# Attention's weight pieces prepared in DRAM during the first ConvFFN, and the queries' swaps issued from ScalarE's queue

## The chip, the cores and the metric

The kernel runs on one core of a Trainium2 chip. The metric is the device time of one execution in microseconds (us), and of several executions the median. Engines are named as in the profile: PE is TensorE, DVE VectorE, ACT ScalarE, POOL GpSimd, and SP is SyncE, which does nothing here but issue DMAs.

## The reference

It is one step of a small decoder over 16 meta tokens, 1024 prompt tokens and 8 sample tokens, with 1024 features: a pooling mixer and a ConvFFN, one shared projection to keys and values, sliding-window attention with sinks, and a second ConvFFN. All is fp32.

```python
def conv_ffn(xs, prefix, w_in, conv_w, conv_b, w_out):
    gu = xs @ w_in                                  # 1024 -> 2 x 2816
    g, u = gu[..., :D_FF], gu[..., D_FF:]
    gp = jnp.concatenate([prefix.astype(g.dtype), g], axis=1)
    c = conv_b
    for k in range(CONV_W):                         # 3 taps
        c = c + gp[:, k:k + S] * conv_w[k]
    h = jax.nn.silu(c) * u
    return h @ w_out, gp[:, -(CONV_W - 1):]
...
    q = (x @ w_q + b_q).reshape(B, L, N_KV_HEADS, GROUP, HEAD_DIM)   # 16 heads of 64
    o = sink_attention(q, k_band, v_band, mask[None, :, None, None], sinks)
    return o @ w_o + b_o
```

## The kernel before

**Exact halves.** An fp32 operand is kept as two parts, a rounded one (hi) and the rest (lo), and a product is made of three matmuls (`mm3`, L116 to L122): hi by hi, hi by lo, lo by hi. Weights arrive in DRAM unsplit. `load_w` (L103) loads 512 KB on SP's queue into one of two `raw` buffers, ACT rounds it into the first half of `w` (L111, CAST), and POOL subtracts (L112) into the second half. Weights of the FFN are split in one piece of 1024 columns, those of the queries (`wq`) and of the output projection (`wo`) in two of 512.

**Stages.** Tokens are columns, in three chunks: 280 columns (meta, samples and 256 of the prompt), 384 and 384. The stages are the mixer (to about 120 us), ConvFFN 1 (about 85 to 840 us, the two interleave), the shared keys and values (about 840 to 890 us), attention (to about 1215 us), and ConvFFN 2 (to the end).

**ConvFFN.** For each of 22 feature tiles f and each chunk c, `ffn1(f, c)` makes the gate product `pg` and the other product `pu` (24 matmuls each); ACT copies `pg` out (`g`, L374 to L376 or L390), POOL and DVE make the convolution (L392 to L394), ACT applies Silu (L398), DVE multiplies by `pu` (L399), ACT rounds the result to `h` (L401) and DVE makes its rest (L402). After f = 3, 4, 6, 8, ... `ffn2(gi, c)` multiplies two tiles of h by `w_wo`, eight products `po` for each chunk; DVE adds them up (for the first group L417 and L418, which also take in the residual; later L420).

**PSUM.** Six banks go round among all these products. A bank that held `pg` comes free when ACT has copied it, one that held `pu` when DVE has multiplied by it. In ffn2 that follows ffn1(f, 2), the first four `po` take the banks of chunks 0 and 1, the fifth takes that of `pg` and the sixth that of `pu` of chunk 2.

**Attention.** For each of 3 chunks and 8 pairs of heads, a query projection `pq` (24 matmuls, L607, spread over the units of the pair before) ends in `Q.finish` (L611 to L628): ACT writes hi of both heads into `q1` (L622), DVE writes lo into `q2` (L627), and since each head also needs the other part in the other 64 partitions, four DMAs swap them, issued on SP's queue (L623 behind ACT, L628 behind DVE). Then each unit of 128 tokens runs scores `s` (PE, L639 and L640), a masked minimum (DVE, L645), exp (ACT, L647), a scale by the reciprocal sum (DVE, L650), a transpose `tp` three units later (PE, L658), its split into `ring` (ACT L660, DVE L661), and the product with the values `av` five units later (PE L676), split into `o` (ACT L681, DVE L683). The output projection `pz` (o_piece, L748) runs beside later units. Eight weights of `wq` and eight of `wo` are needed by every chunk; each chunk loads and splits them again, 48 times in all.

**Order.** Each engine runs its instructions in a fixed order, which a scheduler has set when the program was built; an instruction that waits holds up all behind it on its engine, and a DMA is issued in the order of the engine that issues it. The tag `lt` has five buffers for temporaries of the layer norms, which are idle while the FFN runs.

Of the kernel before, what the change touches and what calls it, by code (L numbers as in the profile page):

```python
# [13 lines left out]
P = 128  # L14
# [13 lines left out]
# prompt blocks (of 128 tokens) per chunk; the first chunk also carries the  # L28
# meta tokens and the sample tokens: columns [meta 16 | samples 8 | prompt]
# [6 lines left out]
# columns alive after the attention: [meta14 meta15 | samples 8 | prompt]  # L36
# [3 lines left out]
# packed per-partition constant columns  # L40
# [7 lines left out]
# constants of the first phase alone  # L48
# [6 lines left out]
def r32(ap):  # L55
    return ap.bitcast(F32)
# [3 lines left out]
def trunk_kernel(ctx: ExitStack, tc: tile.TileContext, ins: dict, outs: dict):  # L60
# [19 lines left out]
    # ------------------------------------------------------------ constants  # L80
# [33 lines left out]

    def mm3(out, wts, movs):
        """out += sum_k w_k^T x_k over exact hi/lo parts (all but lo*lo)."""  # L116
        n = len(wts)
        for k in range(n):
            (wh, wl), (mh, ml) = wts[k], movs[k]
            nc.tensor.matmul(out, lhsT=wh, rhs=mh, start=(k == 0), stop=False)  # L120
            nc.tensor.matmul(out, lhsT=wh, rhs=ml, start=False, stop=False)  # L121
            nc.tensor.matmul(out, lhsT=wl, rhs=mh, start=False, stop=(k == n - 1))  # L122
# [7 lines left out]
    # ----------------------------------------------------------- layer norm  # L130
    def colsum(parts, W, name, on_pe, own=False, split=False, pairs=False, step=KT):
        """mean over all features of 8 [P, W] tiles -> PSUM, on every partition; pauses after every step tiles."""
        ps = bank(f"ps_{name}", "ln")[:, :W]
        if on_pe:
            # fp32 products; with pairs, of sums of two tiles
            n = KT // 2 if pairs else KT
            for k in range(n):
                if pairs:
                    t = hslot([P, W], f"pr{k}_{name}", F32)
                    (nc.gpsimd if k < n // 2 else nc.vector).tensor_tensor(t, parts(2 * k), parts(2 * k + 1), ALU.add)  # L140
                else:
                    t = parts(k)
                nc.tensor.matmul(ps, lhsT=r32(ones), rhs=t, start=(k == 0), stop=(k == n - 1))
            return ps
        s = [None, None]
        for m in range(0, KT, 2):
            # two chains of sums, so that one is ready while the other's last ends
            i = m // 2 % 2
            a, b = parts(m), parts(m + 1)
            eng = nc.vector if split and i else nc.gpsimd  # L150
            if s[i] is None:
                s[i] = a if own else ltmp([P, W], f"s{i}_{name}")
                eng.tensor_tensor(s[i], a, b, ALU.add)
            else:
                eng.tensor_tensor(s[i], s[i], a, ALU.add)
                eng.tensor_tensor(s[i], s[i], b, ALU.add)
            if (m + 2) % step == 0 and m + 2 < KT:
                yield
        s, s1 = s
        nc.gpsimd.tensor_tensor(s, s, s1, ALU.add)  # L160
        sh = ltmp([P, W], f"sh_{name}", F32R)
        sl = ltmp([P, W], f"sl_{name}", F32R)
        nc.scalar.copy(sh, s)
        nc.vector.tensor_tensor(sl, s, r32(sh), ALU.subtract)
        nc.tensor.matmul(ps, lhsT=ones, rhs=sh, start=True, stop=False)
        nc.tensor.matmul(ps, lhsT=ones, rhs=sl, start=False, stop=True)
        return ps
# [10 lines left out]
    def ln_steps(z, W, lni, c, xo, name, out=None, on_pe=False, on_pool=(), lnexp=False, split=False, fin=False):  # L178
        # a list of tiles in the place of x, which gets new ones
# [18 lines left out]
        if lnexp:  # L198
            # both functions share a table set with the softmax's
            nc.scalar.activation(rstd, var, AF.Ln, bias=epsc)  # L200
            nc.scalar.activation(rstd, rstd, AF.Exp, scale=-0.5)
        else:
            nc.scalar.activation(rstd, var, AF.Sqrt, bias=epsc)
            nc.vector.reciprocal(rstd, rstd)
# [37 lines left out]
    # ------------------------------------------------------------ first loads  # L242
# [29 lines left out]
    # ------------------------------------------------------------ pool mixer  # L272
    def pool_chunk(c):
# [22 lines left out]
        def rest(g):  # L296
# [9 lines left out]
            if c == 0:  # L306
                # samples: last w-1 state rows and the token itself
                if w == 2:
                    nc.vector.tensor_tensor(dsm[:, ks], spl[:, ks, :, 2], xst[:, ks], ALU.add)
                else:  # L310
                    st = spl[:, ks] if g == 1 else spt[:, 2 * g - 4:2 * g - 2, :, 16 - w:]
                    nc.vector.tensor_reduce(dsm[:, ks], st, AX.X, ALU.add)
                    nc.vector.tensor_tensor(dsm[:, ks], dsm[:, ks], xst[:, ks], ALU.add)
                nc.vector.scalar_tensor_tensor(dt[:, :, NMETA:NMETA + NS], dsm[:, ks], 1.0 / w, xst[:, ks], ALU.mult, ALU.subtract)
            yield
            # alpha * x
# [12 lines left out]
        for g in range(4):  # L329
            # in this order on the vector engine, whose first groups' loads land first  # L330
            with tc.issue_after(last[g - 1]) if c == 0 and g else nullcontext():
                if g < 3:
                    sums(g)
                r = rest(g)
                next(r)
            next(r, 0)
# [5 lines left out]
    # ------------------------------------------------------------------- FFN  # L342
# [11 lines left out]
    def ffn(L, first_w):  # L354
# [67 lines left out]
        def ffn2_last(gi, c):  # L422
            """the last group: the sums of its first half run while the second half's h is made."""
# [38 lines left out]
        gi = 0  # L462
        for f in range(3, NF - 2):
            win[f + 1] = load_in(f + 1)
            for c in range(NCH):
                ffn1(f, c, *win[f])
            if f == 3 or f % 2 == 0:
                for c in range(NCH):
                    ffn2(gi, c)
                gi += 1  # L470
                load_wo(2 * gi)
                load_wo(2 * gi + 1)
        win[NF - 1] = load_in(NF - 1)
        lns = []
        for c in range(NCH):
# [7 lines left out]
            if c == NCH - 1:  # L483
                exp_tables()
                # the reciprocal root of the chunk before shares this chunk's table set
                for _ in lns[0]:
                    if L == 1:
                        break
# [18 lines left out]
    # ---------------------------------------------------------- phase 1: pool  # L507
# [14 lines left out]
    # ------------------------------------------------- pass-through state rows  # L522
# [7 lines left out]
    # ------------------------------------------------------------ shared K / V  # L530
# [9 lines left out]
    wk = [load_w(ins["wk"][i], f"wk{i}") for i in range(2)]  # L540
    wv = [load_w(ins["wv"][:, 1024 * i:1024 * (i + 1)], f"wv{i}") for i in range(2)]
# [46 lines left out]
    # --------------------------------------------------------------- attention  # L588
    O = {}

    class Q:
        """query projection of head pair t for one chunk, issued in slices."""
# [19 lines left out]
        def finish(self):  # L612
# [5 lines left out]
            # one engine after the other: they take turns at a bank  # L618
            for i in range(2):
# [3 lines left out]
                nc.sync.dma_start(r32(self.q2[os_, i, :]), r32(hi))  # L623
            for i in range(2):
# [3 lines left out]
                nc.sync.dma_start(r32(self.q1[os_, i, :]), r32(lo))  # L628

    def att_s(u, q):  # L630
# [10 lines left out]
        # e = -s with the negated sink as its last column, mx = -max  # L641
# [43 lines left out]
    def load_state(i):  # L685
        """state keys and values of kv heads 2i and 2i+1; slot 0 holds the new token."""
# [7 lines left out]
    def att_virtual(i, kv):  # L694
        """the 8 samples and the last two meta tokens, for kv heads 2i and 2i+1."""
# [49 lines left out]
    def o_weights(c, half, mp):  # L745
        return load_w(ins["wo"][half, mp], f"wo_{c}_{half}_{mp}", pieces=2)

    def o_piece(c, half, m, w, z):  # L748
        """half of the output projection's sum, for output tile m."""
# [6 lines left out]
        if half == 0:  # L756
# [3 lines left out]
            # the sum takes the place of x  # L760
# [5 lines left out]
    def later_kv():  # L766
        """the later chunks' keys and values, made beside the first units."""
# [16 lines left out]
    # slots of 512 columns for the transposed weights; the first query weights pass through  # L784
# [3 lines left out]
    wq = {0: load_w(ins["wq"][0], "wq0", pieces=2, w=early)}  # L788
# [11 lines left out]
    # output projection: (first unit, chunk, half, tile); the weights of a pair of tiles come ahead  # L800
# [21 lines left out]
    for n in range(len(units) + LAG_V + 1):  # L822
        if n < len(units):
            c, t, j = units[n]
            h = heads.index((c, t))
            if h + 1 < len(heads):
                nc_, nt_ = heads[h + 1]
                if j == 0:
                    wq[h + 1] = load_w(ins["wq"][nt_], f"wq{h + 1}", pieces=2, w=early if h == 0 else None)
# [47 lines left out]
def _lay_out(inputs):  # L877
# [5 lines left out]
    def fm(x):  # L883
        """[tokens, features] -> [partition, feature tile, token]"""
# [20 lines left out]
    # heads in pairs: pair 4c+g holds head g of kv head 2c, then of kv head 2c+1  # L905
# [3 lines left out]
    # [half of the pairs, pair of output tiles, partition, (output tile, head pair, column)]  # L909
# [19 lines left out]
    # constants of the shapes alone  # L929
# [46 lines left out]
```

## Time and profile before

| | us |
|---|---|
| median of 3 runs | 2007.79 (2005.25 to 2009.0) |
| profiled execution, first to last instruction (span) | 2004.4 |
| PE busy | 1932.9 (96%) |
| DVE busy | 1263.3 (63%) |
| POOL busy | 813.9 (41%) |
| ACT busy | 712.3 (36%) |

The span is that of one profiled execution. It leaves out what lies before the first and after the last instruction, and is 3.4 us under the median of the runs. Busy shares are means over the whole span; the stages differ widely, so each is read by itself.

### The profile page before, as it was taken

What the parts mean: (1) busy time and instruction counts of PE and PEld (TensorE: products, weight loads), DVE (VectorE), ACT (ScalarE), POOL (GpSimd) and SP (SyncE); (2) the same over time, 40 slices, a digit from 0 to 9 for tenths busy, and PEclk for the clock granted to TensorE, in tenths of its full rate; (3) what the DMA queues carried; (4) which work ended last, traced back from release to release, by engine and by line L of the source; (5) the groups of instructions that cost most, each with busy time, mean ns of one, the idle gap of its engine ahead of it and who ended that gap; (6) DMA issues with size and microseconds to landing.
All of it is one profiled execution on the core that took longest, in us unless ns stands there. A gap on an engine that the chain in (4) does not pass through costs nothing. (4 is left out here: it accounts for less than half of the span.)

```text
span 2004.4 us, 31349 instructions
## 1 busy us (share of the span) xinstructions
PE 1932.9 (96%) x12208; PEld 1896.3 (95%) x12208; DVE 1263.3 (63%) x2367; ACT 712.3 (36%) x1585; POOL 813.9 (41%) x880
## 2 busy tenths in 40 slices
PE   6899999999999999899999989999999999999997
PEld 4699999999999999889999988999999999999996
DVE  7977545454544456887989896675445454544566
ACT  2452122112211221476778784512122112212234
POOL 6752334214321432653464657533143224322333
PEclk9899999999999999999999999999999999999998
DMA  5201111101110111314343322011011011101102
GB/s 194 78 22 43 53 54 63 43 22 64 64 37 27 64 53 34 30 49 148 107 132 102 109 81 85 32 51 55 33 64 55 31 42 63 54 32 43 64 23 65
DMA packets 50422, 123.45 MB, mean 62 GB/s; under 512 B 11481, under 2 KB 25489, under 8 KB 50217
## 3 DMA queue, kind: packets, MB, share of 16 engines
q1 hardware_dynamic: 50272, 121.44, 19.6%
q8 instruction: 96, 1.57, 0.3%
q14 instruction: 54, 0.43, 0.1%
HBM read 108.29 MB, written 7.54 MB: 58 GB/s over the span
## 5 line engine op out<-in xcount | busy, mean ns | idle before, releaser
L112 POOL TENSOR_TENSOR w_wo<-raw_wo,w_wo 128x512 fp32r<-128x512 f32 (+1 forms) x92 | 169.3, 1859 | 550.9 <-ACT w_wo L111 548.0
L121 PE MATMUL pg<-xl,w_g 128*128 128x384 f32 (+2 forms) x1056 | 337.4, 319 | 0.0
L121 PE MATMUL pu<-xl,w_u 128*128 128x384 f32 (+2 forms) x1056 | 336.6, 319 | 0.0
L420 DVE TENSOR_TENSOR acc<-acc,po 128x384 f32<-128x384 f32 (+2 forms) x432 | 222.1, 515 | 173.8 <-PE po L122 170.9
L121 PE MATMUL po<-h,w_wo 128*128 128x384 f32 (+2 forms) x960 | 305.9, 319 | 0.0
L120 PE MATMUL po<-h,w_wo 128*128 128x384 f32 (+2 forms) x960 | 305.7, 318 | 0.0
L122 PE MATMUL po<-h,w_wo 128*128 128x384 f32 (+2 forms) x960 | 305.6, 318 | 0.0
L111 ACT CAST w_wo<-raw_wo 128x512 fp32r<-128x512 f32 (+1 forms) x92 | 71.6, 822 | 422.4 <-PE po L122 417.6
L402 DVE TENSOR_TENSOR h<-c,h 128x280 fp32r<-128x280 f32 (+2 forms) x132 | 147.7, 1119 | 88.3 <-ACT h L401 87.7
L392 POOL TENSOR_SCALAR c<-g,cols 128x384 f32<-128x384 f32 (+1 forms) x110 | 80.2, 729 | 294.6 <-issue 281.6
L121 PEld LDWEIGHTS pg<-xl,w_g 128*128 128x128 f32 x1056 | 198.8, 188 | 0.1
L121 PEld LDWEIGHTS pu<-xl,w_u 128*128 128x128 f32 x1056 | 198.3, 188 | 0.0
L393 DVE SCALAR_TENSOR_TENSOR c<-g,cols,c 128x384 f32<-128x384 f32 (+1 forms) x110 | 67.8, 616 | 194.4 <-POOL c L392 194.4
L122 PEld LDWEIGHTS po<-h,w_wo 128*128 128x128 f32 x960 | 180.4, 188 | 0.0
L120 PEld LDWEIGHTS po<-h,w_wo 128*128 128x128 f32 x960 | 180.3, 188 | 0.0
L121 PEld LDWEIGHTS po<-h,w_wo 128*128 128x128 f32 x960 | 180.1, 188 | 0.0
L398 ACT ACTIVATE c<-c 128x280 f32<-128x280 f32 (+2 forms) x132 | 65.1, 493 | 312.4 <-DVE c L394 277.5
L120 PE MATMUL pg<-xh,w_g 128*128 128x384 f32 (+1 forms) x528 | 170.1, 322 | 0.0
L122 PE MATMUL pg<-xh,w_g 128*128 128x384 f32 (+1 forms) x528 | 169.1, 320 | 0.0
L120 PE MATMUL pu<-xh,w_u 128*128 128x384 f32 (+1 forms) x528 | 168.9, 320 | 0.0
L122 PE MATMUL pu<-xh,w_u 128*128 128x384 f32 (+1 forms) x528 | 168.8, 320 | 0.0
L120 PE MATMUL pg<-xa,w_g 128*128 128x384 f32 (+1 forms) x528 | 168.6, 319 | 0.0
(270 smaller groups left out, 4673.5 us busy)
## 6 DMA issues: line engine op xcount, KB each, us to landing
raw_g<-in_win SPq DMA_DIRECT2D x44, 512.0 KB, 3.5
raw_u<-in_win SPq DMA_DIRECT2D x44, 512.0 KB, 3.5
raw_wo<-in_wout SPq DMA_DIRECT2D x44, 512.0 KB, 3.5
raw_wq<-in_wq SPq DMA_DIRECT2D x24, 512.0 KB, 3.5
raw_wo<-in_wo SPq DMA_DIRECT2D x24, 512.0 KB, 3.6
q<-q SPq DMA_DIRECT2D x64, 96.0 KB, 2.1
praw<-in_xq SPq DMA_DIRECT2D x8, 400.0 KB, 5.4
out_yT<-acc SPq DMA_DIRECT2D x8, 384.0 KB, 2.5
```

Of the source, the lines that this page charges most:

```text
L111: nc.scalar.copy(w[:, 0, s], raw[:, s])
L112: nc.gpsimd.tensor_tensor(w[:, 1, s], raw[:, s], r32(w[:, 0, s]), ALU.subtract)
L120: nc.tensor.matmul(out, lhsT=wh, rhs=mh, start=(k == 0), stop=False)
L121: nc.tensor.matmul(out, lhsT=wh, rhs=ml, start=False, stop=False)
L122: nc.tensor.matmul(out, lhsT=wl, rhs=mh, start=False, stop=(k == n - 1))
L392: nc.gpsimd.tensor_scalar(cc, g[:, 0:n], w0, b, ALU.mult, ALU.add)
L393: nc.vector.scalar_tensor_tensor(cc, g[:, 1:1 + n], w1, cc, ALU.mult, ALU.add)
L398: nc.scalar.activation(ct, ct, AF.Silu)
L402: nc.vector.tensor_tensor(ht[:, 1, :], ct, r32(ht[:, 0, :]), ALU.subtract)
L420: nc.vector.tensor_tensor(a, a, ps, ALU.add)
```

## The change

Twenty weights (2 `wk`, 2 `wv`, 8 `wq`, 8 `wo`) are split once and kept in a DRAM tile `halves`. A generator, `split_ahead`, makes them in 60 pieces (384, 384 and 256 columns of each weight); each piece is loaded by a DMA issued on ACT's queue into an `lt` buffer, rounded by ACT, subtracted by POOL, and stored by two DMAs on ACT's queue. `ffn(0, ...)` takes one piece after each `ffn1` and `ffn2` call from f = 3 on. Keys, values, queries and output projection then load both halves with one DMA of 1 MB (`load_halves`, SP's queue) in the place of `load_w`. Apart from that, the four swaps of each of the 24 query projections are issued on ACT's queue in the place of SP's.

```diff
+    halves = tc.dram_tile([20, P, 2, 1024], F32, name="halves")
+    OWK, OWV, OWQ, OWO = 0, 2, 4, 12
+
+    def split_ahead():
+        srcs = [ins["wk"][i] for i in range(2)] + [ins["wv"][:, 1024 * i:1024 * (i + 1)] for i in range(2)]
+        srcs += [ins["wq"][i] for i in range(8)] + [ins["wo"][i // 4, i % 4] for i in range(8)]
+        for i, src in enumerate(srcs):
+            for a, e in ((0, 384), (384, 768), (768, 1024)):
+                lo = ltmp([P, e - a], f"sl{i}_{a}", F32R)
+                nc.scalar.dma_start(r32(lo), src[:, a:e])
+                hi = ltmp([P, e - a], f"sh{i}_{a}", F32R)
+                nc.scalar.copy(hi, r32(lo))
+                nc.gpsimd.tensor_tensor(lo, r32(lo), r32(hi), ALU.subtract)
+                nc.scalar.dma_start(halves[i][:, 0, a:e], r32(hi))
+                nc.scalar.dma_start(halves[i][:, 1, a:e], r32(lo))
+                yield
+
+    def load_halves(i, name, tag="w", w=None):
+        if w is None:
+            w = pool.tile([P, 2, 1024], F32R, tag=tag, bufs={"w": 4, "wo": 2}[tag], name=f"w_{name}")
+        nc.sync.dma_start(r32(w), halves[i])
+        return w
...
+        ahead = split_ahead() if L == 0 else iter(())
         for f in range(3, NF - 2):
             win[f + 1] = load_in(f + 1)
             for c in range(NCH):
                 ffn1(f, c, *win[f])
+                next(ahead, 0)
             if f == 3 or f % 2 == 0:
                 for c in range(NCH):
                     ffn2(gi, c)
+                    next(ahead, 0)
...
-    wk = [load_w(ins["wk"][i], f"wk{i}") for i in range(2)]
-    wv = [load_w(ins["wv"][:, 1024 * i:1024 * (i + 1)], f"wv{i}") for i in range(2)]
+    wk = [load_halves(OWK + i, f"wk{i}") for i in range(2)]
+    wv = [load_halves(OWV + i, f"wv{i}") for i in range(2)]
...
-                nc.sync.dma_start(r32(self.q2[os_, i, :]), r32(hi))
+                nc.scalar.dma_start(r32(self.q2[os_, i, :]), r32(hi))
...
-                nc.sync.dma_start(r32(self.q1[os_, i, :]), r32(lo))
+                nc.scalar.dma_start(r32(self.q1[os_, i, :]), r32(lo))
...
-        return load_w(ins["wo"][half, mp], f"wo_{c}_{half}_{mp}", pieces=2)
+        return load_halves(OWO + 4 * half + mp, f"wo_{c}_{half}_{mp}")
...
-                    wq[h + 1] = load_w(ins["wq"][nt_], f"wq{h + 1}", pieces=2, w=early if h == 0 else None)
+                    wq[h + 1] = load_halves(OWQ + nt_, f"wq{h + 1}", w=early if h == 0 else None)
```

In the changed kernel the line numbers are some 25 to 28 higher: g is L399 to L401 and L415, Silu L423, h L426, Q.finish's ACT part L650 and its swaps L651 and L656, exp L675, ring L688, o L709. A piece's load is L126, its CAST L128, POOL's subtraction L129, and its stores L130 (hi) and L131 (lo).

**ACT, the end of ffn1(3, 2) and the first ffn2.** Before, ACT's next work behind the last h (`h_3_2`) is the split of the next group's weights (`w_wo_2`), and then the copy of the next `pg`:

```order
L390 COPY g_3_2_1481<-pg_3_2_1430 128x384
L398 ACTIVATE c_3_2_1480<-c_3_2_1480 128x384
L401 CAST h_3_2_1490<-c_3_2_1480 128x384
L111 CAST w_wo_2_1714<-raw_wo_2_1712 128x1024
L111 CAST w_wo_3_1719<-raw_wo_3_1717 128x1024
L374 COPY g_4_0_1783<-pg_4_0_1732 128x16
```

Now pieces (`sl` is a piece as loaded and later its lo, `sh` its hi) stand between Silu and h, and ten CASTs of pieces with their DMAs between h and `w_wo_2`. The rows begin at the same Silu:

```order
L423 ACTIVATE c_3_2_1497<-c_3_2_1497 128x384
L128 CAST sh_0_2968<-sl_0_2966 128x384
L126 DMA sl_384_3036<-in_wq 128x384
L130 DMA halves<-sh_0_2968 128x384
L426 CAST h_3_2_1507<-c_3_2_1497 128x384
L128 CAST sh_384_3038<-sl_384_3036 128x384
L131 DMA halves<-sl_0_2966 128x384
L126 DMA sl_768_3106<-in_wq 128x256
L130 DMA halves<-sh_384_3038 128x384
L131 DMA halves<-sl_384_3036 128x384
L128 CAST sh_768_3108<-sl_768_3106 128x256
L126 DMA sl_0_3191<-in_wq 128x384
```

The scheduler has moved the pieces ahead of where the generator is called: all 60 stand between ACT's rstd of the mixer's last layer norm (which starts at 119.54 us in the trace before) and its copy of g of f = 6, chunk 0 (270.22 us); 22 of them stand ahead of `h_3_2`. The load of a piece always stands right behind the CAST of the one before it, so that one load is under way at a time. A second run of ten CASTs stands between `h_4_2` and `w_wo_4`. PE's order in the first ConvFFN is the same in both kernels.

**ACT, one query projection in the last chunk (pair 3).** Before, two splits of weights stand between ACT's writing of the query's hi and the work of the next units:

```order
L622 ACTIVATE q_2_3_11106<-pq_3_11105,cols 64x384 x2
L111 CAST w_wo_1_3_11345<-raw_wo_1_3_11343 128x512 x2
L660 CAST ring<-tp_1_2_11256 128x512
L647 ACTIVATE e_2_2_11242,mx_2_2_11243<-e_2_2_11242,mx_2_2_11243 128x257 x2
L681 CAST o_1_11263<-av_1_0_11264 64x128 x2
L111 CAST w_wo_0_0_11482<-raw_wo_0_0_11480 128x512 x2
L660 CAST ring<-tp_2_0_11325 128x512
```

Now the splits are gone, and the swaps stand in ACT's order, the later two behind DVE's lo:

```order
L650 ACTIVATE q_2_3_11347<-pq_3_11346,cols 64x384 x2
L651 DMA q_2_3_11348<-q_2_3_11347 64x384 x2
L675 ACTIVATE e_2_2_11478,mx_2_2_11479<-e_2_2_11478,mx_2_2_11479 128x257 x2
L688 CAST ring<-tp_1_2_11492 128x512
L709 CAST o_1_11499<-av_1_0_11500 64x128 x2
L656 DMA q_2_3_11347<-q_2_3_11348 64x384 x2
L688 CAST ring<-tp_2_0_11556 128x512
```

In some pairs nothing stands between the two groups of swaps, in others one to three instructions do.

## Rows read from the trace of the kernel before

**Rows 1.** Windows by stage: busy time of each engine, then granted clock.

```profile
core 0: us, PE busy (x) PEld busy (x) DVE busy (x) ACT busy (x) POOL busy (x), PEclk, DMA share, GB/s
150.00:800.00 650.00, 649.86 (x4117) 649.60 (x4116) 342.70 (x543) 137.53 (x269) 208.71 (x230) 1.00 0.14 48
800.00:850.00 50.00, 42.81 (x240) 41.79 (x239) 42.95 (x62) 22.35 (x39) 29.95 (x30) 0.97 0.28 29
850.00:925.00 75.00, 70.01 (x515) 68.52 (x514) 60.13 (x133) 50.84 (x119) 32.93 (x35) 0.98 0.28 79
925.00:1150.00 225.00, 219.77 (x1560) 216.25 (x1559) 203.48 (x602) 174.92 (x497) 123.16 (x159) 0.98 0.40 118
1150.00:1225.00 75.00, 63.48 (x384) 60.59 (x383) 67.24 (x167) 57.26 (x147) 46.46 (x46) 0.93 0.25 75
```

**Rows 2.** Waits of PE in 800 to 850 us: total, times, longest.

```profile
PE po L433 <- DVE c L399: 4.4, 1, 4.4
```

**Rows 3.** Timeline of DVE: start, duration, line, operation; near 834 and 1018 us.

```profile
834.80 2.49 DVE L393 SCALAR_TENSOR_TENSOR c<-g,cols,c 128x384 f32<-128x384 f32 x1
...
838.48 0.60 DVE L394 SCALAR_TENSOR_TENSOR c<-g,cols,c 128x384 f32<-128x384 f32 x1
...
1015.91 1.69 DVE L650 TENSOR_SCALAR e<-e,mx 128x256 f32<-128x256 f32 x2
...
1021.49 0.61 DVE L650 TENSOR_SCALAR e<-e,mx 128x256 f32<-128x256 f32 x2
```

**Rows 4.** Timeline of POOL in the same two places.

```profile
834.49 2.39 POOL L112 TENSOR_TENSOR w_wv<-raw_wv,w_wv 128x1024 fp32r<-128x1024 f32 x1
...
1016.11 2.65 POOL L112 TENSOR_TENSOR w_wo<-raw_wo,w_wo 128x512 fp32r<-128x512 f32 x2
```

**Rows 5.** Groups of instructions by form, 870 to 1200 us: count, busy us, mean ns.

```profile
L650 DVE TENSOR_SCALAR e<-e,mx 128x256 f32<-128x256 f32 x124 | 62.2, 543 | 1.2
L112 POOL TENSOR_TENSOR w_wo<-raw_wo,w_wo 128x512 fp32r<-128x512 f32 x44 | 57.3, 1322 | 30.1 <-ACT w_wo L111 27.4 <-issue 2.6
...
L111 ACT CAST w_wo<-raw_wo 128x512 fp32r<-128x512 f32 x44 | 25.1, 617 | 2.8 <-PE pz L122 1.6 <-DMA raw_wo<-in_wo 0.9
```

**Rows 6.** Waits of PE, 870 to 1225 us.

```profile
PE tp L658 <- DVE e L650: 4.0, 2, 3.6
...
PE s L639 <- DMA q<-q: 1.6, 2, 0.8
```

**Rows 7.** DMA issues: KB of each, median us from issue to landing.

```profile
raw_g<-in_win SPq DMA_DIRECT2D x44, 512.0 KB, 3.5
...
q<-q SPq DMA_DIRECT2D x64, 96.0 KB, 2.1
...
q<-q SPq DMA_DIRECT2D x32, 64.0 KB, 2.3
...
raw<-in_xq SPq DMA_DIRECT2D x2, 288.0 KB, 3.2
```

**Rows 8.** Windows where the pieces stand now: columns as in the first group.

```profile
119.50:177.00 57.50, 57.50 (x349) 57.50 (x348) 37.27 (x45) 23.64 (x44) 28.66 (x31) 1.00 0.17 56
177.00:198.10 21.10, 21.10 (x133) 21.10 (x132) 19.89 (x45) 0.01 (x1) 0.00 (x0) 1.00 0.00 1
198.10:222.60 24.50, 24.50 (x158) 24.50 (x157) 14.89 (x18) 8.31 (x15) 13.47 (x13) 1.00 0.27 86
222.60:244.10 21.50, 21.50 (x136) 21.50 (x135) 11.91 (x24) 0.03 (x1) 0.00 (x0) 1.00 0.00 1
```

**Rows 9.** Timeline of ACT from the last g of f = 3; idle time in brackets.

```profile
171.61 0.48 ACT L390 COPY g<-pg 128x384 f32<-128x384 f32 x1 [3.04 <-PE pg L122]
174.34 0.52 ACT L398 ACTIVATE c<-c 128x384 f32<-128x384 f32 x1 [2.25 <-DVE c L394]
176.37 0.51 ACT L401 CAST h<-c 128x384 fp32r<-128x384 f32 x1 [1.51 <-DVE c L399]
198.09 2.00 ACT L111 CAST w_wo<-raw_wo 128x1024 fp32r<-128x1024 f32 x2 [21.21 <-PE po L122]
```

**Rows 10.** Timeline of DVE at the start of the first ffn2.

```profile
175.78 0.55 DVE L399 TENSOR_TENSOR c<-c,pu 128x384 f32<-128x384 f32 x1 [1.56 <-PE pu L122]
...
180.35 0.45 DVE L417 SCALAR_TENSOR_TENSOR acc<-xh,po 128x280 f32<-128x280 f32 x1
180.72 0.44 DVE L418 SCALAR_TENSOR_TENSOR acc<-xl,acc 128x280 f32<-128x280 f32 x1
```

**Rows 11.** Timeline of SP at one query projection: issue of its swaps.

```profile
1151.73 1.11 SPq L623 DMA_DIRECT2D q<-q  x2
1153.98 1.12 SPq L628 DMA_DIRECT2D q<-q  x2
```

More of the change, by code (lines that the diff above doesn't have):

```diff
@@ L787, in trunk_kernel @@
     early = ring[:, :4, :].rearrange("p (a b) c -> p a (b c)", a=2)
-    wq = {0: load_w(ins["wq"][0], "wq0", pieces=2, w=early)}
+    wq = {0: load_halves(OWQ, "wq0", w=early)}
     qs = {heads[0]: Q(0, 0, wq[0])}
```

## The prediction

> **What bounds the kernel now.** I read the busy times by stage first, because the change adds work to one stage and takes it from another [rows 1]. From 150 to 800 us, inside the first ConvFFN, PE is busy for 649.86 of 650 us: nothing can be won there, and whatever makes PE wait is lost outright. DVE (343), POOL (209) and ACT (138) have room on the mean. From 800 us on it looks different. PE idles 7.2 us of the 50 at the end of the FFN, 5.0 of 75 around keys and values, 5.2 of 225 in attention, and 11.5 of the last 75 before the second FFN: 28.9 us in all. DVE is the nearest rival there (203 of 225, 67 of 75), ACT is next (175 and 57). So up to some 29 us lie in that stretch, and a little more where the granted clock is below 1 (0.93 in the last 75 us).
>
> Next, what makes PE wait there. At 836 us PE stands still for 4.4 us for DVE's product with `pu` [rows 2]. DVE was late because one step of the convolution (L393) took 2.49 us, where its neighbour L394 of the same form took 0.60 [rows 3]; it ran while POOL subtracted for `w_wv`, from 834.49 for 2.39 us [rows 4]. In attention the pattern repeats: two scalings (L650) take 1.69 us while POOL subtracts (1016.11, 2.65 us) and 0.61 us where it doesn't [rows 3, 4]. The largest wait of PE in attention is for L650: 4.0 us [rows 6].
>
> A rule bears on that. The Trainium skill, "SBUF — State Buffer", section "Who interferes with whom", says that VectorE and GpSimd share one pair of ports as an exclusive lock: an operation of VectorE with two inputs from SBUF, or in a two-port mode, fully blocks against one of GpSimd. The two rows agree. By that rule alone one would expect all of DVE's loss to come back.
>
> **What the change removes.** It removes 100 CASTs and 100 subtractions after 830 us: 44 + 44 of each in attention by these groups (the ones of `wq` read like those of `wo`), 25.1 us of ACT and 57.3 us of POOL for each 44 [rows 5]. ACT gets some 50 us back, POOL some 115. DVE gets back what POOL's lock cost: 124 scalings took 62.2 us, and at the undisturbed 0.61 us for two they take 37.8, so 24 us, and a few more for other operations [rows 3, 5]. What does PE get of it? Below, nothing: DVE's time is not on PE's path for most of the 225 us, where PE idles 5.2. Above, all idle time from 850 us on, 21.7 us [rows 1]. Scores wait for PE and exps for DVE in a ring of units, and 300 us of it hold 24 us of DVE, 8%; where DVE is the bound (the last 75 us, and waits as of [rows 6]) this is worth that share. I take **-10**, half of the ceiling. At the boundary, the wait of 4.4 us loses the excess of L393 (1.9 us) and part of what stood before it in DVE's queue; POOL's reductions of the layer norm also start 2.4 us earlier. I take **-3** (0 to -5).
>
> **What it adds in the first FFN.** A piece is a load, a CAST of 128x384 (0.5 us on ACT by the CAST of h, which has that shape [rows 9]), a subtraction and two stores. One load is under way at a time, and it is issued right behind the CAST of the piece before, so a piece takes as long as its load takes to land and little more. No load of 192 or 128 KB is in the trace: 96 KB land in 2.1 us, 288 KB in 3.2 [rows 7]. That brackets it; by interpolation 192 KB take 2.65 and 128 KB about 2.3, a mean of 2.5 over the three pieces of a weight. With 0.1 us for the hand-over I take 2.6 us a piece, 2.1 to 3.3 as bounds.
>
> The Trainium skill, "DMA: Bandwidth & Descriptors", section "Anatomy of one DMA", gives a fit of 2.0 us plus the bytes at 436 GB/s for another kind of issue. By it, as an estimate, 192 KB take 2.45 us, and the sum below would be about 3 us lower.
>
> Now the queue. Behind each piece on ACT stand the FFN's own copies, Silus and rounds, and these hand work to PE. 22 pieces stand ahead of `h_3_2`, from 119.5 us on: 22 x 2.6 = 57.2 us, in a stretch of 57.5 us up to the end of that h [rows 8, 9]. The load chain alone just fits, but 23 of ACT's own instructions stand between them that wait for PE or DVE (before each the row shows 1.5 to 3.0 us of idle time [rows 9]), and where a load stands behind such a wait the chain stops. At half a microsecond each that is some 11 us. So Silu and h of f = 3, chunk 2, come 11 us late. What is late next is the bank of `pu`: DVE's product with it ended at 176.3 us, and the sixth `po`, which takes that bank, was summed at 180.35, having run for about 0.8 us: 3.2 us of slack [rows 10]. PE stalls **8 us**.
>
> In the first ffn2 DVE is busy for 19.9 of 21.1 us with sums of which every second (L418) reads two operands from SBUF [rows 8, 10], and POOL, which was idle, gets eight to ten subtractions of about 1 us (half of 1024 columns took 1.3 [rows 5]). By the locks seen above DVE loses 5 us or so; some lies in the stall: **+3** (0 to +8).
>
> Ten CASTs in a row then have to fit between h and `w_wo_2`, where ACT idled 21.2 us [rows 9]: 26 us for 21 plus the stall. ACT starts f = 4 still late, and there another 12 pieces share 24.5 us with 8.3 us of its own work [rows 8]. Between two ffn1s of one f a bank is needed only after another whole chunk, some 16 us later, so no stall there; but at the start of the second ffn2 the 3 us of slack count again. I put the lag there at 7.6 us: a stall of **4** more. In f = 5 no ffn2 follows, the last pieces end with f = 6, and the rest of the FFN has ACT busy for a fifth of its time [rows 1]. The sum is **+15**; its lower bound is 2 (2.1 us a piece, all waits covered by flight), its upper 35 (3.3 us a piece: 22 x 0.7 = 15 us more at the first stall, and a few at the second).
>
> **What moving the swaps does.** On SP two swaps take 1.1 us to issue [rows 11], so 96 of them add 53 us to ACT, as much as the CASTs it loses: ACT doesn't become lighter. The second pair waits for DVE's lo: on SP it came 2.25 us behind the first, 1.1 us after that was issued, and ACT's exps, ring and o stand behind it. 24 heads x 1.1 us is 27 us of standing; a unit's exp is used by PE three units later, which covers most. I charge one in six, **+4.5**, with 0 (all covered) and +15 (half of it on the path, as DVE too waits for exps) as bounds. A gain is possible: SP's queue no longer holds loads behind a wait for swaps, and PE waits 1.6 us for swaps at most [rows 6]. Against it a rule: the same page, section "Issuing engines are not separate DMA queues", says that issuing from several engines saves only the issuer's time. The rows show swaps landing in 2.1 us among loads [rows 7], and no run here shows them from ACT.
>
> The 52 loads of 1 MB carry twice the bytes on DMA engines that are 40% busy in attention [rows 1]; they need a free `w` buffer where before only `raw` was needed ahead, but save a CAST and a subtraction behind it (about 0.6 + 1.3 us for half [rows 5]). I cost them at nothing: SP issues them a head ahead, and the matmuls of that head hide them. With that cover gone, half a microsecond of waiting for every third of the 48 would be 8 us more.
>
> **Sum.** +15 -3 -10 +4.5 = +6.5 us. The profiled span is 2004.4 and the median 2007.8, 3.4 us outside the first and last instruction, which the change doesn't touch: **2014 us**.
>
> **Rivals.** *Faster:* loads land in 2.1 to 2.3 us, pieces fit into ACT's idle time, and the FFN loses 2 to 4 us; attention recovers 12 to 20 of 28.9. Time 1992 to 2001. For it speak the short swaps [rows 7] and the saturated DVE; against it the 23 waits in the chain. It decides at about 2.2 us a piece, where 22 pieces leave 9 us for them. *The lock's end doesn't reach PE:* in attention the DVE time given back is only idle time, swaps cost what is left, and the FFN loses 2 to 6: 2006 to 2012. For it speaks that PE loses only 5.2 of 225 us today. *Slower:* loads share queue and engines with the FFN's own and with 120 stores and take 3 us or more; the first stall grows to 15 to 20 us, the second to 8: 2024 to 2043.
>
> **Chances.** The forecast (2004 to 2022) 0.46, the faster case 0.30, no effect in attention 0.11, long loads 0.13. Measurement tells a change of 0.2%, 4 us, from none, so bounds are 2003.8 and 2011.8. The forecast case is slower in 0.37 and same in 0.09; no effect is same in 0.08, faster in 0.01, slower in 0.02. Faster 0.31, same 0.17, slower 0.52. The range takes in the faster case but its lowest end and long loads but theirs: 1994 to 2036. The forecast's own range is 2004 to 2022.
>
> **What would show it.** PE waiting for `pu`'s bank near 179 us, 5 to 12 us long, ACT in a row of CASTs each 2.6 us after the last, a second stall after f = 4; L650's mean near 0.35 us; POOL nearly empty in attention; PE's idle time from 850 to 1225 us near 15. Wrong if no PE wait over 3 us lies before 300 us, or if pieces follow each other in over 3 us, or if L650 stays above 0.5 us with POOL empty.

## The result and the profile after

The changed kernel takes 2038.1 us (median of 4 runs, 2034.0 to 2040.2) against 2008.4 us (the kernel before, again over 4 runs): a ratio of 1.0147, interval 1.0133 to 1.0162. It is slower, by some 30 us where 6.5 were forecast, and 2 us outside the range. The profiled execution's span is 2036.7 us against 2004.4.

The windows of the changed kernel by stage, with the three places where PE now stalls in the first ConvFFN (columns as in [rows 1]):

```profile
177.00:197.00 20.00, 8.26 (x37) 7.03 (x36) 6.91 (x11) 6.42 (x14) 9.86 (x14) 0.61 0.59 182
197.00:240.00 43.00, 43.00 (x264) 43.00 (x263) 29.56 (x54) 12.09 (x24) 23.56 (x22) 0.98 0.62 206
240.00:253.00 13.00, 3.98 (x22) 3.20 (x20) 5.01 (x7) 3.88 (x8) 6.54 (x10) 0.75 0.66 211
253.00:320.00 67.00, 66.86 (x407) 66.86 (x408) 26.86 (x44) 20.17 (x41) 36.88 (x37) 0.97 0.62 200
320.00:331.00 11.00, 5.11 (x35) 4.30 (x34) 5.75 (x11) 3.69 (x8) 2.67 (x8) 1.00 0.12 42
331.00:840.00 509.00, 508.85 (x3221) 508.59 (x3220) 258.51 (x415) 107.78 (x211) 162.24 (x181) 1.00 0.14 46
...
837.00:887.00 50.00, 46.68 (x261) 45.97 (x260) 38.60 (x65) 20.99 (x39) 22.24 (x29) 0.93 0.40 71
887.00:962.00 75.00, 68.00 (x500) 66.46 (x500) 58.63 (x135) 42.78 (x107) 16.94 (x23) 0.98 0.35 114
962.00:1187.00 225.00, 216.01 (x1529) 213.32 (x1529) 178.70 (x589) 134.37 (x415) 32.78 (x83) 0.98 0.61 204
1187.00:1262.00 75.00, 67.99 (x427) 63.84 (x426) 64.70 (x176) 51.36 (x139) 29.44 (x33) 0.98 0.36 119
```

From 177 to 840 us three short stretches hold nearly all of PE's idle time: 11.7, 9.0 and 5.9 us, each at the start of an ffn2 (after f = 3, 4 and 6). In the last four rows, the stages of [rows 1] moved by 37 us, PE idles 3.3, 7.0, 9.0 and 7.0 us: 26.3 where it was 28.9. DVE is busy for 24.8 us less in the 225 us of attention and POOL for 90 us less, but PE idles there more than before.

How far the first ConvFFN has fallen behind at its end is read from one matmul behind the same wait of 2.82 us near its end. In the kernel before, and then in the changed one, from the timeline of PE:

```profile
814.77 1.51 PE L433 MATMUL po<-h,w_wo 128*128 128x384 f32 x7 [2.82 <-DVE acc L441]
```

```profile
851.41 1.33 PE L458 MATMUL po<-h,w_wo 128*128 128x384 f32 x3 [2.82 <-DVE acc L466]
```

That is 36.6 us, of which 4.3 are won back by the end of the kernel in this pair of executions. So the first ConvFFN holds the whole loss. The windows that end at these two matmuls, before and after, show what it is made of:

```profile
119.50:814.77 695.27, 692.31 (x4361) 691.73 (x4359) 373.92 (x585) 160.14 (x310) 228.62 (x252) 1.00 0.14 46
```

```profile
119.50:851.41 731.91, 701.44 (x4360) 697.29 (x4359) 373.44 (x585) 187.14 (x369) 284.47 (x312) 0.98 0.27 87
```

PE's idle time grows from 3.0 to 30.5 us, which is 27.5, and PE is busy for 9.1 us longer with the same matmuls.

The chain at the largest stall, from the timelines of ACT, DVE and PE of the changed kernel (start, duration, then in brackets the idle time before it and what ended it):

```profile
179.20 0.44 ACTq L131 DMA_DIRECT2D halves<-sl  x1
...
184.33 0.34 ACTq L126 DMA_DIRECT2D sl<-in_wq  x1
...
187.00 0.51 ACT L128 CAST sh<-sl 128x384 fp32r<-128x384 f32 x1 [5.64 <-DMA sl<-in_wq]
187.03 0.34 ACTq L126 DMA_DIRECT2D sl<-in_wq  x1
187.54 0.33 ACTq L130 DMA_DIRECT2D halves<-sh  x1
187.91 0.52 ACT L423 ACTIVATE c<-c 128x384 f32<-128x384 f32 x1 [0.40 <-ACT sh L128]
```

```profile
188.47 0.55 DVE L424 TENSOR_TENSOR c<-c,pu 128x384 f32<-128x384 f32 x1 [4.48 <-ACT c L423]
```

```profile
182.47 0.43 PE L147 MATMUL po<-h,w_wo 128*128 128x280 f32 x1
189.08 0.60 PE L145 MATMUL po<-h,w_wo 128*128 128x280 f32 x1 [6.18 <-DVE c L424]
...
198.81 0.29 PE L145 MATMUL po<-h,w_wo 128*128 128x280 f32 x1
```

Read from below: PE waits 6.18 us for a bank that DVE's product frees, DVE waits for ACT's Silu, the Silu stands behind the CAST of a piece, and that CAST waited 5.64 us for the piece's load. More than half of that was not flight: the load was issued at 184.33 us, 3.7 us behind the start of the CAST before it, when the store issued at 179.20 had landed (by its semaphore at 184.31) and so freed one of the five `lt` buffers. It isn't even chunk 2 that stalls PE here but chunk 1: ACT is a whole chunk behind. The matmuls between the stalls take 0.43 us and later 0.29 again: behind the waits PE runs at the lower of its two clock levels, 1.2 GHz in the place of 2.4 (granted clock 0.61 from 177 to 197 us and 0.75 from 240 to 253, but 1.00 in the third stall), which costs on top.

In attention the waits of PE have changed hands (total us, times, longest), against [rows 6]:

```profile
PE s L667 <- DMA q<-q: 5.6, 4, 2.5
PE s L667 <- ACT q L650: 3.8, 2, 3.1
PE pq L635 <- DMA ring<-halves: 3.2, 1, 3.2
...
PE pq L635 <- DMA w_wq<-halves: 1.0, 1, 1.0
```

The wait of 4.0 us for DVE's scaling is gone; waits for the queries' swaps have come. The swaps land late, and the 1 MB loads are long (DMA issues of the changed kernel, columns as in [rows 7]; such a median is taken over those transfers whose landing the profile shows, 23 of these 64 swaps and 31 of the 64 in the kernel before):

```profile
w_wo<-halves SPq DMA_DIRECT2D x24, 1024.0 KB, 5.5
...
q<-q ACTq DMA_DIRECT2D x64, 96.0 KB, 5.4
...
sl<-in_wq ACTq DMA_DIRECT2D x16, 192.0 KB, 2.7
```

### The profile page after: what moved, and what is told of

It is laid out like the page before. It is cut to its first block, busy times and chain, and to the rows that moved or that the text cites. A ratio compares the mean times of both kernels' runs of the same rounds, so it can differ in the third digit from the quotient of the medians.

```text
span 2036.7 us, 31542 instructions
## 1 busy us (share of the span) xinstructions
PE 1941.5 (95%) x12208; PEld 1901.5 (93%) x12208; DVE 1231.3 (60%) x2367; ACT 683.7 (34%) x1545; POOL 735.7 (36%) x840
## 4 chain that ended last, share of the span: by engine, by line
PE 72%; DVE 6%; issue 3%; DMA 2%; ACT 1%; POOL 1%; DVEq 0%; ACTq 0%; POOLq 0%
PE pg L145 7%; PE pg L147 7%; PE pg L146 7%; PE pu L146 7%; PE pu L145 7%; PE pu L147 7%; PE po L145 6%; PE po L146 6%; PE po L147 6%; PE pq L635 3%; PE av L704 1%; PE po L458 1%; DMA q<-q 1%; PE pz L145 1%; PE pz L146 1%
## 5 line engine op out<-in xcount | busy, mean ns | idle before, releaser
L112 POOL TENSOR_TENSOR w_wo<-raw_wo,w_wo 128x1024 fp32r<-128x1024 f32 x44 | 105.8, 2423 | 460.6 <-ACT w_wo L111 460.5
L145 PEld LDWEIGHTS po<-h,w_wo 128*128 128x128 f32 x960 | 182.6, 190 | 29.6 <-DVE c L424 23.1
L147 PEld LDWEIGHTS po<-h,w_wo 128*128 128x128 f32 x960 | 182.8, 190 | 0.0
L146 PEld LDWEIGHTS po<-h,w_wo 128*128 128x128 f32 x960 | 182.6, 190 | 0.0
L111 ACT CAST w_wo<-raw_wo 128x1024 fp32r<-128x1024 f32 x44 | 44.2, 1047 | 373.4 <-PE po L147 372.4
L145 PE MATMUL pg<-xa,w_g 128*128 128x384 f32 (+1 forms) x528 | 168.7, 320 | 0.0
L147 PE MATMUL pg<-xa,w_g 128*128 128x384 f32 (+1 forms) x528 | 168.5, 319 | 0.0
```

Of the source, the lines that this page charges most:

```text
L111: nc.scalar.copy(w[:, 0, s], raw[:, s])
L112: nc.gpsimd.tensor_tensor(w[:, 1, s], raw[:, s], r32(w[:, 0, s]), ALU.subtract)
```

## The experiments

**One part alone, and one part undone.** The first kernel is the one before with only the swaps moved, the second the changed one with the swaps moved back (one of the two lines is shown; that of lo changes alike):

```diff
-                nc.sync.dma_start(r32(self.q2[os_, i, :]), r32(hi))
+                nc.scalar.dma_start(r32(self.q2[os_, i, :]), r32(hi))
```

> The kernel before, with only the 96 swaps moved to ScalarE's queue. Theory A (the swaps landed in 5.4 us instead of 2.1 because loads of 1 MB are under way beside them, not because of the queue): here swaps land in about 2.1 us and the time is 2006 to 2013 us. Rival B (ScalarE's queue makes a swap late): they land in about 5 us, PE waits for q, 2013 to 2022 us.

Measured: 2011.5 us, ratio 1.0020 (1.0008 to 1.0031). Swaps land in 2.1 us. ACT's queue doesn't make a swap late; the move costs about 4 us by itself.

> The changed kernel with the swaps back on SP's queue; the first ConvFFN keeps its stalls. Theory A: swaps still share the DMA engines with 1 MB loads and land in 4 to 6 us, time 2034 to 2044 us. Rival B: they land in about 2.1 us, attention is 5 to 10 us shorter, 2027 to 2033 us.

Measured: 2040.3 us, ratio 1.0162 (1.0138 to 1.0187). Issued from SP they land just as late, as its DMA issues show:

```profile
q<-q SPq DMA_DIRECT2D x64, 96.0 KB, 5.0
```

So the halves delay the swaps on either queue. The rule of the Trainium skill, "DMA: Bandwidth & Descriptors", section "Issuing engines are not separate DMA queues", agrees: 5.4 us from ACT, 5.0 from SP, and 2.1 from either without the halves.

**The first ConvFFN without ACT's and POOL's share.** Each piece is copied from DRAM to DRAM by SP:

```diff
-                lo = ltmp([P, e - a], f"sl{i}_{a}", F32R)
...
-                nc.scalar.dma_start(halves[i][:, 1, a:e], r32(lo))
+                nc.sync.dma_start(halves[i][:, 0, a:e], src[:, a:e])
+                nc.sync.dma_start(halves[i][:, 1, a:e], src[:, a:e])
```

> The changed kernel, where the pieces are copied from DRAM to DRAM by SP, each behind a load of the FFN: ScalarE and GpSimd do nothing for them, and both halves hold the unsplit weight, so the low part is left out. Bytes moved stay about the same. Theory A (the first ConvFFN loses its 36 us to waits in ScalarE's queue): no PE wait over 1 us from 150 to 350 us, and 2000 to 2006 us. Rival C (the DMA traffic of the pieces delays the FFN's own loads): stalls stay in part, 2012 to 2035 us.

Measured: 2000.9 us, ratio 0.9970 (0.9956 to 0.9985). The stalls are gone with the work on ACT and POOL; so the same bytes, spread by SP from 156 to 594 us, delay nothing. Packed into 200 us, as the change has them, their traffic was not tested alone; but in the changed kernel's trace no wait of PE in that stretch is for a load.

**The same work, paced.** The generator's pieces are bound behind the h of the call before them, the load goes one piece ahead and the store of lo one piece behind:

```diff
+            hc = nc.scalar.copy(ht[:, 0, :], ct).ins
...
+                hc = ffn1(f, c, *win[f])
+                two = f % 2 == 0 and c == NCH - 1
+                with tc.issue_after(hc):
+                    for _ in range(3 if two else 1):
+                        next(ahead, 0)
```

> The changed kernel with the same 60 pieces, but each bound behind the h of one ffn1 call (three behind the last before an ffn2), its load issued one piece earlier and its low part stored one piece later, so that ScalarE waits for no load; pieces end at about f = 18. Theory A (order and waits, not the amount of work): the stalls go, 2000 to 2007 us. Rival D (the work itself: 60 subtractions on GpSimd block VectorE, 120 stores): 2012 to 2035 us.

Measured: 1998.5 us, ratio 0.9955 (0.9940 to 0.9971): faster than the kernel before. Its window over the FFN holds nearly all of the 60 CASTs and subtractions (59 and 57 instructions more on ACT and POOL than [rows 1]), and PE loses nothing:

```profile
150.00:800.00 650.00, 649.85 (x4117) 649.59 (x4116) 347.49 (x543) 162.81 (x328) 263.88 (x287) 1.00 0.30 96
```

**Pacing without loading ahead**, to tell the place of the pieces from the waits for their loads. The generator is the change's own; only the binding of the kernel above is kept.

> The changed kernel, each piece bound behind the h of one ffn1 call as in the paced one, but loaded, rounded, subtracted and stored there in one go, as the change does it; ScalarE waits for each load and each subtraction. Theory A, first part (the crowding ahead of two ffn2 is what costs): 1998 to 2004 us. Second part (each wait for a load in ScalarE's queue costs): stalls of 1 to 2 us at every second f, 2010 to 2025 us.

Measured: 2000.5 us, ratio 0.9956 (0.9939 to 0.9973), level with the paced one. ACT still waits for every load and subtraction, one piece at a time; the only wait of PE from 120 to 800 us:

```profile
PE po L459 <- DVE c L424: 0.2, 1, 0.2
```

The second part of the theory, that each wait in ACT's queue costs, has fallen. What costs is that pieces stand packed ahead of an ffn2, so that the waits add up: the binding is all that differs here from the changed kernel.

**The split with no use**, to price it alone: the paced generator in the kernel before, attention untouched.

> The kernel before with the paced split added to the first ConvFFN, whose stored halves nobody reads; attention and swaps as before. Theory A (paced, the split costs nothing, and all that the paced kernel gains comes from what the halves spare later): 2005 to 2009 us. Rival D (60 subtractions and 180 transfers cost PE something even so): 2010 us or more.

Measured: 2009.2 us, ratio 1.0010 (0.9999 to 1.0022), between the two ranges. Paced, the split costs between nothing and 4 us; the profiled execution shows no wait of PE at all from 120 to 800 us. The paced kernel's 9 us come from what the halves spare later.

**Paced, with the swaps on SP.**

> The paced kernel of before with the swaps on SP's queue again. Theory A (a swap is late because of the 1 MB loads, and the move to ScalarE's queue costs some 3 to 5 us, as it did alone): 1992 to 1997 us, swaps still land in about 5 us. Rival B (behind the loads on SP the swaps are held up more): 1999 to 2005 us.

Measured: 2001.5 us, ratio 0.9966 (0.9953 to 0.9979). Theory A fails here, and the time lies in rival B's range: beside the 1 MB loads, moving the swaps to ACT's queue costs nothing, and may save 2 us (0.9955 against 0.9966, intervals that overlap). PE waits 8.9 us for q instead of 6.5. Alone the move costs, with the loads it doesn't.

**Fewer bytes: only wo in halves, wq split in attention as before.**

```diff
-    wq = {0: load_halves(OWQ, "wq0", w=early)}
+    wq = {0: load_w(ins["wq"][0], "wq0", pieces=2, w=early)}
```

> As the paced kernel with swaps on SP's queue, but only wk, wv and wo go through DRAM in halves (36 pieces); wq is loaded whole and split by ScalarE and GpSimd in attention, as before. Bytes per head pair fall from 2 MB to 1.5 MB, half of the subtractions come back. Theory A (late swaps cost what VectorE's relief gives): swaps land in 3 to 4 us, 1993 to 1999 us, near the kernel with all in halves. Rival (VectorE's relief is worth more than the swaps' delay): 1998 to 2004 us.

Measured: 1997.2 us, ratio 0.9941 (0.9927 to 0.9954); swaps land in 4.1 us, and PE still waits 10.3 us for q. The time is what theory A gave, but it lies 4 us under the kernel with all in halves although PE waits longer for q, so that gain comes from elsewhere; from where is not shown.

**Twice the bytes in the kernel before.**

```diff
+        ld = nc.sync.dma_start(raw, src).ins
+        if name[:2] == "wq" or name[:3] == "wo_":
+            with tc.issue_after(ld):
+                nc.sync.dma_start(spare[len(twice) % 8][:, 0, :], src)
```

> The kernel before, where each load of a query or output weight in attention is followed on SP's queue by a copy of the same 512 KB from DRAM to DRAM that nobody uses; the rest is untouched. Theory A (bytes under way delay the swaps): swaps land in 4 to 6 us, PE waits 5 us or more for q, 2010 to 2020 us. Rival B: landing stays near 2.1 us and time within 2004 to 2009 us.

Measured: 2008.1 us, ratio 1.0001 (0.9989 to 1.0012). Twice the bytes cost no time, and PE waits 3.4 us for q. The median landing of the 96 KB swaps is 2.0 us, that of the 64 KB swaps of the first chunk 4.6 where it was 2.3 [rows 7]. These medians rest on few swaps, 5 of 64 and 6 of 32, and they don't refute theory A. Of the five, four land in 2.0 us; the fifth was issued 1.3 us behind a copy and takes more than twice that (DMA issues from 1055 to 1058 us):

```profile
q<-q SPq DMA_DIRECT2D x2, 96.0 KB, 4.5
```

By the times of issue, 20 of the 96 swaps here follow within 3 us on a load or copy of 512 KB; in the kernel before 17 follow so closely on such a load, in the changed kernel 67 on one of 1 MB. So this kernel moves twice the bytes, but rarely while a swap is on its way. What it shows is that bytes moved at other times don't matter here.

The order of issue tells the cases apart. In the kernel before, the timeline of SP shows the load behind the swaps:

```profile
1091.83 1.11 SPq L623 DMA_DIRECT2D q<-q  x2
1094.24 1.12 SPq L628 DMA_DIRECT2D q<-q  x2
1095.76 0.33 SPq L105 DMA_DIRECT2D raw_wq<-in_wq  x1
```

In the changed kernel, SP's load and then ACT's query and swaps:

```profile
1143.15 0.32 SPq L137 DMA_DIRECT2D w_wo<-halves  x1
```

```profile
1143.16 1.18 ACT L650 ACTIVATE q<-pq,cols 64x384 fp32r<-64x384 f32 x2 [1.03 <-PE pq L635]
1143.76 1.12 ACTq L651 DMA_DIRECT2D q<-q  x2
```

A load into `raw` was released by POOL's subtraction. A load straight into `w` is released by the last matmul that reads the old weight: by the trace, 20 of the 46 loads of `w_wq` and `w_wo` by a matmul of a query projection, as the one above, 19 by one of the output projection. The same matmul of the query releases ACT's hi and so the swaps. So 1 MB is under way just when the swaps start. The kernel before shows the same in small: its 96 KB swaps with no load issued in the 6 us ahead of them land in 2.0 to 2.1 us (16 swaps), those issued within 3 us behind a load of 512 KB in 2.0 to 4.0, median 2.6 (6 swaps).

**The order turned round.** Each 1 MB load in attention is bound behind the swaps issued last, in the kernel with all halves, and in the one with wo alone:

```diff
+        with tc.issue_after(swap[0]) if swap[0] is not None else nullcontext():
+            nc.sync.dma_start(r32(w), halves[i])
```

> The paced kernel with the swaps on SP, and each 1 MB load in attention bound behind the swaps that the program issued last, so that a load that comes free by the same last matmul no longer goes ahead of the swaps. Theory E (the swaps are late because the load and the swaps are released at the same moment, not because of bytes as such): swaps land in 2 to 3 us, PE waits under 3 us for q, 1993 to 1998 us. Rival F (bytes: landing stays at 5 us): 1999 to 2004 us. Rival G (loads now come late and PE waits for weights instead): over 2002 us with waits for w.

Measured: 2132.5 us, ratio 1.0626 (1.0611 to 1.0641). Of theory E the landing comes true, swaps in 2.1 us with all bytes still there; its time does not, because G comes true as well and PE waits for weights. From its DMA issues and its waits of PE:

```profile
q<-q SPq DMA_DIRECT2D x64, 96.0 KB, 2.1
```

```profile
PE pq L652 <- DMA w_wq<-halves: 74.4, 17, 7.6
PE pz L159 <- DMA w_wo<-halves: 18.8, 5, 5.0
```

> The same binding in the paced kernel that takes only wk, wv and wo in halves. Theory E: the 10 us that PE waits for q there fall to under 3, 1988 to 1995 us. Rivals F and G: 1996 to 2003 us.

Measured: 1993.6 us, ratio 0.9935 (0.9922 to 0.9948), in theory E's range and the fastest of all by its median, with an interval that overlaps that of the kernel with wo alone and no binding. Swaps land in 2.1 us, and PE's waits for q fall from 10.3 us to one of 4.3, where under 3 was expected:

```profile
PE s L684 <- DMA q<-q: 4.3, 1, 4.3
```

> The paced kernel with all weights in halves and swaps on SP, where only the loads of wo are bound behind the swaps and those of wq keep their place. If the late swaps are the whole of what holds attention back there, swaps land in 2 to 4 us and the time is 1992 to 1997 us, level with the kernel that takes only wo in halves. If weights of 1 MB come late as soon as any is held (rival G), PE waits for w and the time is over 2003 us.

Measured: 2019.5 us, ratio 1.0063 (1.0047 to 1.0080): rival G. Swaps of 96 KB land in 2.1 us, but PE waits 11.9 us for w_wo. With wq loaded whole as 512 KB, PE has no such wait. That loads of 1 MB for both weights leave no room to hold one back is the reading of this pair; no run separates it from the order in which SP's queue holds these loads.

## Why the prediction was wrong, point by point

**The step that failed** is the size of the first ConvFFN's term: +15, measured 36.6 [rows 8, 9, 10 and the two matmuls above]. Its mechanism was right: the pieces packed ahead of the ffn2s, one load at a time, banks freed late through ACT's Silu and DVE's product, the first two stalls where they were placed. The upper bound for this term, 35, was passed.

Three parts of it were too small. *The lag.* A piece was put at 2.6 us. In the run of ten that follows h that is nearly so: the first CAST starts at 198.25 us and the last at 223.23, 2.8 us each. But ahead of h the 22 CASTs run from 121.72 to 195.22 us, 3.5 us each. By the times of issue and landing in the trace, 61.0 of these 73.5 us are the flight of 21 loads, 2.9 us each instead of 2.5; five of them took 3.7 to 4.4, four of which went out within 1.3 us of a 512 KB load of the FFN. The other 12.5 us are ACT's own work and waits, near the 11 that were charged; among them two waits for a buffer whose store had not landed, 2.3 and 3.7 us behind the CAST before, which the prediction left out. h of f = 3, chunk 2, starts at 196.13 instead of 176.37 us [rows 9], 19.8 us late and not 11:

```profile
121.72 0.50 ACT L128 CAST sh<-sl 128x384 fp32r<-128x384 f32 x1
...
195.22 0.51 ACT L128 CAST sh<-sl 128x384 fp32r<-128x384 f32 x1 [0.57 <-DMA sl<-in_wq]
...
196.13 0.51 ACT L426 CAST h<-c 128x384 fp32r<-128x384 f32 x1 [0.40 <-ACT sh L128]
198.25 0.51 ACT L128 CAST sh<-sl 128x384 fp32r<-128x384 f32 x1 [1.61 <-DMA sl<-in_wq]
...
223.23 0.51 ACT L128 CAST sh<-sl 128x384 fp32r<-128x384 f32 x1 [2.35 <-DMA sl<-in_wq]
...
319.15 0.41 ACT L128 CAST sh<-sl 128x256 fp32r<-128x256 f32 x1 [4.15 <-DMA sl<-in_wo]
```

*The stalls.* 8 + 4 were forecast; the windows show 11.7 and 9.0, and a third of 5.9 after f = 6, where the prediction saw no ffn2 in the way because it sought one after f = 5. The last CAST (319.15 us) even stands behind the copies of g of f = 6, chunk 0 (314.49 to 314.61 us), and not ahead of them, and so right at that ffn2. *The clock.* Nothing was charged for PE running at the lower clock behind a stall. The same matmuls keep PE busy for 9.1 us longer, most of it in the first two stalls, where those of 280 columns take 0.43 us instead of 0.29. With the 27.5 us of added idle time this makes up the 36.6. The term for DVE against POOL in the first ffn2 (+3) isn't seen: from 197 to 240 us PE is busy throughout.

**Attention and boundary** were forecast at -3 - 10 + 4.5 = -8.5. In the pair of profiles they came to -4.3, but one pair can't tell these apart: from the first of the two matmuls to the second ConvFFN the kernel before takes 408.0 us in its profile, and the kernel with the unused split, whose attention is the same, 415.9. By the medians the whole change is +29.7, less 36.6 is -6.9; and the paced kernel is some 11 us faster than the one with the unused split (0.9955 against 1.0010). So this sum was not far off. Its parts were: the boundary's wait of 4.4 us [rows 2] is gone, as forecast. DVE's scalings (L650) got back 20.2 us over the whole kernel where 24 were worked out, with a mean of 393 ns and not the 305 of an undisturbed pair; all of DVE is busy for 24.8 us less in the 225 us of attention [rows 1, 5]. Before, then after:

```profile
L650 DVE TENSOR_SCALAR e<-e,mx 128x256 f32<-128x256 f32 x128 | 64.9, 548 | 1.2
```

```profile
L678 DVE TENSOR_SCALAR e<-e,mx 128x256 f32<-128x256 f32 x128 | 44.7, 393 | 1.2
```

That agrees with the lock in the Trainium skill, "SBUF — State Buffer", section "Who interferes with whom". But PE got only part of it. In these profiles its wait of 4.0 us for the scalings [rows 6] is gone, and the last 75 us idle for 7.0 us instead of 11.5; in the 225 us before them PE idles for 9.0 us instead of 5.2, 5.0 of it for swaps, which cost 1.6 before, and 3.8 for ACT's hi of the query. The prediction costed the 1 MB loads at nothing, as hidden by a head's matmuls. PE waited 4.2 us for such loads in all, 3.2 of it at one query projection, and beside that they delayed the swaps from 2.1 to 5.4 us.

**The move of the swaps** was put at +4.5. Alone it costs about 4 us (1.0020); beside the halves it costs nothing that could be measured.

**The rivals.** Long loads (2024 to 2043 us, 0.13) gave the right time, and in part for its reason: loads that share the queue and the engines with the FFN's own took 2.9 us each ahead of the first ffn2, nearly its 3, and a first stall that leaves PE 17 us late is what it put there (a matmul that started at 180.80 us starts at 198.02). Behind h a piece took 2.8 us, and the second and third stalls with the lower clock make up the rest. What would have shown the prediction wrong, pieces more than 3 us apart, is what happened ahead of the first ffn2.

**The time outside the span.** The prediction put 3.4 us before the first and after the last instruction. The changed kernel's profiled execution took 2038.5 us with a span of 2036.7, so 1.8; the rest of the 3.4 is that the median and the span before came from different executions. The forecast, a difference added to the median, doesn't change by it.

## What to carry to other kernels

Work put on an engine that is idle for most of a stage (ACT was busy for 138 of 650 us) can still stall the engine that is the bound, if the order packs it ahead of the place where that engine's buffers are short: the same 60 pieces cost 36.6 us packed and nothing that shows as a stall when one stood behind each h. When a helper's results are loaded straight into the buffer that a matmul frees, look at what else the same matmul frees: here the load and the short swaps started together, and putting the swaps first gave the kernel with the lowest median, but only with half of the weights loaded in this way; with all of them PE waited for weights instead. A relief of one engine is worth what is left when the next wait ends: write down which that will be.

## What the runs showed that was not expected

A swap of 96 KB lands in 2.1 us or in over 5, depending on what has been issued just before it: with the same 1 MB loads, 5.1 us in the paced kernel, where most swaps follow closely on one, and 2.1 when the loads go behind. Copies of 512 KB that double the bytes, but are rarely under way beside a swap, leave the time as it was. The issuing queue made no difference to the landing. And a chain of pieces through five buffers can wait for its own stores: three of the 60 loads were issued only when a store had landed 4.1 to 5.6 us after its issue.
